# A diffusion trunk layer in fp32 on one core: first stage by blocks of 128 features, one modulation row as a column, six first products ahead of the FFN

## The chip, the core and the metric

The kernel runs on one core of a Trainium2 chip, in one launch. The metric is the device time of that launch in microseconds (us); the runs shown give its median. TensorE is called PE here, VectorE DVE, ScalarE ACT, GpSimd POOL, and SyncE, which here only issues transfers, SP.

## The reference

One layer of a latent diffusion trunk, all fp32, with T = 1024 latent tokens, 256 context tokens, D = 1024 features and a hidden FFN width of 2816:

```
mod   = silu(c) @ w_ada + b_ada          # six vectors of D: sh1 sc1 gt1 sh2 sc2 gt2
mod_c = silu(c_ctx) @ w_ada + b_ada      # the context uses its first two
hc = rmsnorm(ctx, g_pre_mix) * (1 + csc1) + csh1
hl = rmsnorm(x, g_pre_mix) * (1 + sc1) + sh1
states = context_mixer(hc @ w_in)        # only the final scan states
yl = latent_mixer(hl @ w_in, states)     # GLA | 2-D Fourier | conv + RG-LRU
x = x + gt1 * rmsnorm(yl @ w_out, g_post_mix)
hf = rmsnorm(x, g_pre_ffn) * (1 + sc2) + sh2
x = x + gt2 * rmsnorm((silu(hf @ w_gate) * (hf @ w_up)) @ w_down, g_post_ffn)
```

`w_in` has columns for Q, K, V, a decay (DEC), an output gate (OG), the Fourier part (F), and the two inputs of the RG-LRU (RX, RG).

## The kernel before

**Products.** PE multiplies in a reduced format, so every operand is split into a rounded upper half and the rest, its lower half (`split`: ACT casts, DVE or POOL subtracts, line 92), and every product is three matmuls, hi·hi, hi·lo and lo·hi (`mm3`, lines 84 to 86). A row of the trace with L84, L85 or L86 is one of these three, whichever product it belongs to; the name of what is written (`z`, `zn`, `zvc`, `zkc`, `zc`, `o_ps`, `prod`, `dn`) tells which.

**Order and memory.** A scheduler puts the instructions of each engine into an order and inserts the waits. Tiles come from two pools, `pg` (43 tiles of 4 KB per partition) and `hp` (13 of 2 KB), handed out in program order; psum has four banks `mm` and four `aux`. All loads go through SP's queue, in the order in which they stand in the program (`load`); at most eight transfers of the queues are under way at once, since they rotate through eight semaphores.

**First stage** (to about 61 us). Context rows are loaded and normed, `ada_half` computes half of the first two modulation vectors for latent and context tokens from eight loads of 512 KB (64 matmuls with 32 rows, line 154), `columns` brings them into columns, one number per feature (line 200), and `modulate` (lines 189 to 191) turns transposed tokens into `h * scale + shift`, with ACT, and its two halves, with DVE. Context products (`zvc`, `zkc`, then `zc`) are put between the two halves of the modulation; x's rows are loaded behind that, 0 to 3 and then 4 to 7, and transposed (line 181). Then `z_v0` (psum name `zn`), and, later, `z_k` and `z_rx` do the columns V, K and RX of the latent tokens.

**Modulation rows.** Of the other four vectors each is summed by DVE (`ada_row`, line 671, eight steps over D with a load of 512 KB each) and spread over all partitions by two products with ones (`row_ps`, line 682), times a gain row (line 690). This is so for gt1 and for g_pre_ffn·(1 + sc2); the shift sh2 becomes a column by eight small products (`col_ps`, line 676). The calls `ada_step(n)` say where in the program these steps stand: 4, 4, 9, 0, 11, 0. The second row is used in `x_product`, where DVE computes x·(1/rms)·row (line 1034); `x_transposed` (line 1042) transposes that, and ACT adds sh2 as its bias (line 1049). The row for gt2 is summed after block 3 of the FFN.

**FFN's border.** Gate and up products follow Strassen and Winograd: the tokens' two halves of features and of tokens give seven operands, a11, a12, s1, s2, s3, s4, a22 (`operand`, `put`, `sums`), and each of 22 blocks of hidden features has two products with a11 and a12 (`first`) and five with the others (`rest`). `sums(n)` needs tokens n and n + 4, so the last of them wait for the mixer's last rows. Sums and lower halves are made by DVE (lines 937, 1065, 1068) and POOL (1071, 1074, 937). While they run, PE does `first` for `EARLY` = 3 blocks. `t_split` (lines 1122 to 1127) combines the weights of a block for `rest`; their upper halves are called `wa_hi` and `wb_hi`, the weights of `first` `b_hi`. The loop over f then does `rest(f)` with one `first` behind it:

```
    for f in range(NFF):
        new = begun < NFF and begun - f <= (EARLY if f < 2 else EARLY - 1)
        if new:
            ff_gate(begun)
            ff_up(begun)
        wn = t_split(f + 1) if f + 1 < NFF else None
...
        rest(f, w)
        if new:
            ff_b1(begun)
            first(begun)
            begun += 1
```

Of the kernel before, what the change touches and what calls it, by code (L numbers as in the profile page):

```python
# [16 lines left out]
P = 128  # L17
# [21 lines left out]
def tile_trunk(ctx: ExitStack, tc: tile.TileContext, A: dict):  # L39
# [118 lines left out]
    Bcol = pool.tile([P, KB, 2], F32, name="Bcol")  # L158
# [35 lines left out]
    def columns(h, ps):  # L194

        sb = hp((P, 256), name="ada_sb")
        S.copy(sb, ps[:, 0:256])
        pc = (aux if h else mm)("ada_pc")[:, 0:16].rearrange("p (m q) -> p m q", q=8)
        for m in range(2):
            PE.matmul(pc[:, m], sb[:, m * P:(m + 1) * P], sel, start=True, stop=True)  # L200
        pcv = pc.rearrange("p m (i j w) -> p i j m w", i=2, j=2)

        def col4(c0):
            return sml[:, c0 + 4 * h:c0 + 4 * h + 4].rearrange("p (j m) -> p j m", j=2).unsqueeze(3).to_broadcast([P, 2, 2, 2])

        Av, Bv = (t[:, 4 * h:4 * h + 4, :].rearrange("p (j m) w -> p j m w", j=2) for t in (Acol, Bcol))
        V.tensor_add(Av, pcv[:, 1], col4(S_BSC))
        V.scalar_tensor_tensor(Av, Av, 1.0, col4(S_GPM), op0=ALU.add, op1=ALU.mult)
        V.tensor_add(Bv, pcv[:, 0], col4(S_BSH))

    load(cm, A["cmat"])
    cb = [row_block(A["ctx"], i * P) for i in range(2)]
    ada_ps = ada_half(0)
    for xb in cb:
        norm(xb)
    cT = list(transposed(cb))
# [74 lines left out]

    raws = w_N_load([(C_V, 256), (C_DEC, 32)])
    columns(0, ada_ps)
    hc = [[pg((P, 4, TC), F32R, f"hc{s}{i}") for i in range(2)] for s in range(2)]

    def mod_c(h):
        return modulate(cT[4 * h:4 * h + 4], 1, lambda kk: hc[0][kk // 4][:, kk % 4, :], lambda kk: hc[1][kk // 4][:, kk % 4, :])

    mod_c(0)
    w_v = [w_N_split(raws, G)]  # L300
    w_k_raw = [w_T_load(C_K)]
    zvc = [mm("zvc") for _ in range(2)]
    zkc = [mm("zkc") for _ in range(2)]

    def v_c(ks):
        for m in range(2):
            for k in ks:
                mm3(zvc[m][:, 0:288], *(hc[s][k // 4][:, k % 4, m * P:(m + 1) * P] for s in range(2)), *w_v[0][k], k == 0, k == KB - 1)

    v_c(range(4))  # L310
    ada_ps = ada_half(1)
    w_k_raw.append(w_T_load(C_K + P))
    w_k = [split(r, (P, KB, P), eng=G) for r in w_k_raw]
    xb0 = [row_block(A["x"], i * P) for i in range(2)]
    columns(1, ada_ps)
    started = mod_c(1)
    v_c(range(4, KB))
    for p in range(2):
        z_c(w_k[p], range(KB), zkc[p])
    w_rx_raw = w_T_load(C_RX)  # L320
    xb0 += [row_block(A["x"], i * P) for i in range(2, 4)]


    wdec_raw, wdec = hp(name="wdec_raw"), hp((P, 512), F32R, "wdec")
    load(wdec_raw, A["wdec"])
    with tc.issue_after(started.ins):
        S.copy(wdec, wdec_raw)
        V.tensor_sub(wdec[32:64, :], wdec_raw[32:64, :], wdec[32:64, :].bitcast(F32))
        w_rx = [split(w_rx_raw, (P, KB, P))]
        for xb in xb0:  # L330
            norm(xb)
# [33 lines left out]
    for m in range(2):  # L365
        v0_parts(zdt_c, m, vNc[0][:, m, :], zvc[m])
# [1117 lines left out]
```

## Time and profile before

| | before |
|---|---|
| median of 3 runs | 1133.83 us (1131.55 to 1134.39) |
| the profiled execution | 1134.18 us, span 1132.4 us |
| PE busy | 1078.5 us (95%) |
| DVE, ACT, POOL busy | 810.4, 490.2, 83.6 us |
| PE's longest waits | 10.1 us (start), 9.7 us (first block that needs all operands), 5.0 us (modulation row) |

A wait is the idle time of an engine before an instruction, put down to what came last. A row of the timeline is a run of like instructions; its first number is the start, the second the time to the end of the last one. PE's matmuls are pipelined, so the spacing of starts and not a row's length is what one costs.

### The profile page before, as it was taken

What the parts mean: (1) busy time and instruction counts of PE and PEld (TensorE: products, weight loads), DVE (VectorE), ACT (ScalarE), POOL (GpSimd) and SP (SyncE); (2) the same over time, 40 slices, a digit from 0 to 9 for tenths busy, and PEclk for the clock granted to TensorE, in tenths of its full rate; (3) what the DMA queues carried; (4) which work ended last, traced back from release to release, by engine and by line L of the source; (5) the groups of instructions that cost most, each with busy time, mean ns of one, the idle gap of its engine ahead of it and who ended that gap; (6) DMA issues with size and microseconds to landing.
All of it is one profiled execution on the core that took longest, in us unless ns stands there. A gap on an engine that the chain in (4) does not pass through costs nothing.

```text
span 1132.4 us, 15040 instructions
## 1 busy us (share of the span) xinstructions
PE 1078.5 (95%) x5547; PEld 900.1 (79%) x5547; DVE 810.4 (72%) x1370; ACT 490.2 (43%) x931; POOL 83.6 (7%) x93
## 2 busy tenths in 40 slices
PE   4899998999899999959999999999999999999997
PEld 2799896776689888838878888888888888888886
DVE  3474698477588466797879777768777668967794
ACT  3452675466373355663314332333323247554251
POOL 2210000103100011370000000000000000000100
PEclk8899999999999999979999999999999999999999
DMA  9802312222427222361283242424232468767572
GB/s 328 306 20 67 120 38 56 48 56 71 167 75 243 75 93 94 112 167 57 93 276 106 78 136 84 121 75 139 85 114 81 157 218 315 267 216 231 181 283 75
DMA packets 119970, 156.42 MB, mean 138 GB/s; under 512 B 8276, under 2 KB 70996, under 8 KB 119896
## 3 DMA queue, kind: packets, MB, share of 16 engines
q1 hardware_dynamic: 106536, 128.72, 34.9%
q10 hardware_dynamic: 13360, 26.75, 7.0%
q8 instruction: 43, 0.70, 0.3%
q14 instruction: 31, 0.25, 0.1%
HBM read 124.50 MB, written 28.57 MB: 135 GB/s over the span
## 4 chain that ended last, share of the span: by engine, by line
PE 83%; DVE 6%; DMA 4%; ACT 3%; issue 2%; POOL 1%; SPq 0%; DVEq 0%; POOLq 0%; ACTq 0%
PE prod L84 11%; PE prod L85 11%; PE prod L86 11%; PE dn L85 6%; PE dn L84 6%; PE dn L86 6%; PE z L84 3%; PE z L85 3%; PE z L86 3%; PE o_ps L85 3%; PE o_ps L86 3%; PE o_ps L84 3%; PE zn L85 3%; PE zn L86 3%; PE zn L84 2%; DMA wraw<-in_w_in 2%
## 5 line engine op out<-in xcount | busy, mean ns | idle before, releaser
L85 PE MATMUL dn<-dr,dl 128*128 128x512 f32 (+1 forms) x319 | 121.8, 382 | 0.0
L86 PE MATMUL dn<-dr,dl 128*128 128x512 f32 (+1 forms) x319 | 121.8, 382 | 0.0
L84 PE MATMUL dn<-dr,dl 128*128 128x512 f32 (+1 forms) x319 | 118.7, 382 | 0.0
L85 PE MATMUL zn<-w_lo,hl 128*128 128x256 f32 (+1 forms) x256 | 74.1, 292 | 0.0
L84 PE MATMUL zn<-w_hi,hl 128*128 128x256 f32 (+1 forms) x256 | 73.2, 289 | 0.0
L86 PE MATMUL zn<-w_hi,hl 128*128 128x256 f32 (+1 forms) x256 | 72.9, 288 | 0.0
L84 PE MATMUL prod<-a,b_hi 128*128 128x512 f32 x176 | 69.5, 395 | 1.4 <-ACT b_hi L91 1.4
L84 PEld LDWEIGHTS dn<-dr,dl 128*128 128x128 f32 x319 | 60.0, 188 | 11.7
L85 PE MATMUL prod<-a,b_hi 128*128 128x512 f32 x176 | 69.3, 393 | 0.0
L86 PEld LDWEIGHTS dn<-dr,dl 128*128 128x128 f32 x319 | 60.0, 188 | 11.7
L85 PEld LDWEIGHTS dn<-dr,dl 128*128 128x128 f32 x319 | 60.0, 188 | 11.5
L84 PE MATMUL prod<-s,wb_hi 128*128 128x512 f32 x176 | 68.9, 391 | 0.0
L86 PE MATMUL prod<-s,wb_lo 128*128 128x512 f32 x176 | 68.5, 389 | 0.0
L85 PE MATMUL prod<-s,wb_hi 128*128 128x512 f32 x176 | 68.5, 389 | 0.0
L86 PE MATMUL prod<-a,b_lo 128*128 128x512 f32 x176 | 67.9, 390 | 0.0
L84 PE MATMUL z<-hl,w_hi 128*128 128x512 f32 x160 | 65.5, 409 | 1.0 <-ACT on L605 1.0
L85 PE MATMUL z<-hl,w_hi 128*128 128x512 f32 x160 | 64.0, 400 | 0.0
L86 PE MATMUL z<-hl,w_lo 128*128 128x512 f32 x160 | 63.8, 399 | 0.0
L1189 ACT CAST dl<-h 128x512 fp32r<-128x512 f32 x77 | 47.8, 620 | 35.7 <-issue 20.6
L1190 DVE TENSOR_TENSOR dl<-h,dl 128x512 fp32r<-128x512 f32 x77 | 53.3, 692 | 13.6 <-ACT dl L1189 13.6
L1122 ACT CAST b<-wf_raw 128x512 fp32r<-128x512 f32 x22 | 13.7, 622 | 113.6 <-PE prod L86 105.7
L85 PE MATMUL o_ps<-wo_lo,yh 128*128 128x512 f32 x128 | 49.9, 392 | 0.0
(368 smaller groups left out, 2800.8 us busy)
## 6 DMA issues: line engine op xcount, KB each, us to landing
ada_raw<-in_w_ada SPq DMA_DIRECT2D x48, 512.0 KB, 6.3
h<-hd SPq DMA_DIRECT2D x77, 256.0 KB, 5.0
wd_raw<-in_w_down SPq DMA_DIRECT2D x77, 256.0 KB, 4.8
hd<-c ACTq DMA_DIRECT2D x55, 256.0 KB, 2.0
wf_raw<-in_w_gate SPq DMA_DIRECT2D x25, 512.0 KB, 3.9
wf_raw<-in_w_up SPq DMA_DIRECT2D x22, 512.0 KB, 4.4
wraw<-in_w_in SPq DMA_DIRECT2D x16, 512.0 KB, 4.6
xb<-in_x SPq DMA_DIRECT2D x8, 512.0 KB, 8.1
```

The lines of the kernel that those rows point to most:

```text
L84: PE.matmul(out, lh, rh, start=start, stop=False)
L85: PE.matmul(out, lh, rl, start=False, stop=False)
L86: return PE.matmul(out, ll, rh, start=False, stop=stop)
L1122: S.copy(hi, u[:, 4:8])
L1189: S.copy(t[:, 0, :], raw)
L1190: V.tensor_sub(t[:, 1, :], raw, t[:, 0, :].bitcast(F32))
```

## The change

Three parts.

**First stage.** x rows 0 to 3 are loaded first, through ACT's queue. The modulation weights come in eight blocks of 128 features, each two loads (shift and scale) with rows of 512 B, and the columns K and RX of `w_in` in four pairs of blocks of 128 rows. For each block: four transposes, 16 matmuls of 32x128, one small column product, `modulate`, and 12 products into four psum banks, which hold K and RX of the first 512 tokens. The products of the context, a short series of small DVE operations (`softplus`) and the second half of x stand behind that, and splits that POOL did go to DVE.

```
...
+    xb0 = [pg(name="xb") for _ in range(4)]
+    for i, xb in enumerate(xb0):
+        nc.scalar.dma_start(xb, A["x"][i * P:(i + 1) * P, :])
...
+    def ada_load(b):
+
+        raws = []
+        for i in range(2):
+            raw = pg((P, KB, P), name="ada_raw")
+            c = i * D + b * P
+            load(raw, A["w_ada"][:, c:c + P].rearrange("(k p) n -> p k n", p=P))
+            raws.append(raw)
+        return raws
+
+    def ada_part(raws):
+
+        ps = aux("ada_ps")
         for k in range(KB):
-            raw = pg((P, 2, 512), name="ada_raw")
-            load(raw, A["w_ada"][k * P:(k + 1) * P, 0:2 * D].rearrange("p (i n) -> p i n", i=2)[:, :, h * 512:(h + 1) * 512])
             for i in range(2):
-                for j in range(2):
-                    q = 32 * (2 * i + j)
-                    PE.matmul(ps[q:q + 32, 0:256], s32[:, k, :], raw[:, i, j * 256:(j + 1) * 256], start=k == 0, stop=k == KB - 1)
+                g = 32 * (2 * i + k % 2)
+                PE.matmul(ps[g:g + 32, 0:P], s32[:, k, :], raws[i][:, k, :], start=k < 2, stop=k >= KB - 2)
         return ps
...
+    def z_block(b):
+        for (hi, lo), ps in zip(w4, z4):
+            mm3(ps, hi[:, b, :], lo[:, b, :], hl[0][0][b // 2][:, b % 2, :], hl[1][0][b // 2][:, b % 2, :], b == 0, b == KB - 1)
...
+    w4_split()
+    for b in range(KB):
+        kps = [next(x0_T)]
+        columns(b, ada_part(a_raw.pop(b)))
+        modulate(kps, 0, lambda kk: hl[0][0][kk // 2][:, kk % 2, :], lambda kk: hl[1][0][kk // 2][:, kk % 2, :])
+        if b:
+            z_block(b - 1)
+        if b % 2:
+            w4_split()
+    softplus()
+    w_v = [w_N_split(v_raws)]
+    z_block(KB - 1)
...
+    z_v0([0, 1, 2, 3])
     for xb in xb1:
         norm(xb)
+    mod_half(1, xb1)
+    cb = [row_block(A["ctx"], i * P) for i in range(2)]
...
+    z_v0([4, 5, 6, 7])
...
```

PE's order at the start of the program, before: transposes of the context (`xT_ps`), half the modulation (`ada_ps`, 32 rows by 256 features), the column products (`ada_pc`), and then context products.

```order
L181 MATMUL xT_ps<-cm,xb 128x128 x4
L154 MATMUL ada_ps<-ada_raw,s_73 32x256 x4
L181 MATMUL xT_ps<-cm,xb 128x128 x12
L154 MATMUL ada_ps<-ada_raw,s_73 32x256 x28
L200 MATMUL ada_pc<-cm,ada_sb 128x8 x2
L84 MATMUL zvc<-w_hi,hc_219 128x288 x2
L85 MATMUL zvc<-w_lo,hc_219 128x288
```

And now, where `xT_ps` are transposes of x and `z` the products of K and RX:

```order
L196 MATMUL xT_ps<-cm,xb 128x128 x3
L168 MATMUL ada_ps<-ada_raw,s_83 32x128
L196 MATMUL xT_ps<-cm,xb 128x128
L168 MATMUL ada_ps<-ada_raw,s_83 32x128 x15
L214 MATMUL ada_pc<-sel_96,ada_sb 128x4
L196 MATMUL xT_ps<-cm,xb 128x128 x4
L168 MATMUL ada_ps<-ada_raw,s_83 32x128 x16
L214 MATMUL ada_pc<-sel_96,ada_sb 128x4
L196 MATMUL xT_ps<-cm,xb 128x128 x4
L168 MATMUL ada_ps<-ada_raw,s_83 32x128 x14
L84 MATMUL z<-hl_97,w_hi 128x512 x4
```

The first products of the latent tokens now stand right behind the modulation of the third block, and those of the context behind all eight.

**Rows.** g_pre_ffn·(1 + sc2) becomes a column too, and `x_transposed` applies it as ACT's scale; ACT then also does x·(1/rms). The steps stand at 8, 8, 1, 7 and 9, and the row for gt2 at blocks 10 and 11 of the FFN.

```
...
+    def scale_column(ps):
+        g8 = hp((P, P), name="g8")
+        load(g8[0:KB, :], A["g_pre_ffn"].rearrange("(k p) -> k p", p=P))
+        PE.transpose(ps[:, 16:16 + KB], g8[0:KB, :], ident[0:KB, 0:KB])
+        V.tensor_copy(sc2, ps[:, 16:16 + KB])
+        V.scalar_tensor_tensor(sc2, ps[:, 0:KB], 1.0, sc2, op0=ALU.add, op1=ALU.mult)
 
     def all_rows():
         yield from ada_row(2 * D, times_row("g_post_mix", 0.0))
-        yield from ada_row(4 * D, times_row("g_pre_ffn", 1.0))
-        yield from ada_row(3 * D, None)
+        yield from ada_row(4 * D, scale_column, False)
+        yield from ada_row(3 * D, shift_column, False)
...
-            V.scalar_tensor_tensor(xn[:, hs], xr[:, hs], r2, sc2[:, hs], op0=ALU.mult, op1=ALU.mult)
+            S.mul(xn[:, hs], xr[:, hs], r2)
...
-                S.activation(x[:, kk, :], ps[:, k * P:(k + 1) * P], AF.Identity, bias=sh2[:, kk:kk + 1])
+                S.activation(x[:, kk, :], ps[:, k * P:(k + 1) * P], AF.Identity, bias=sh2[:, kk:kk + 1], scale=sc2[:, kk:kk + 1])
...
```

PE's order at the end of the products for RG (`z`), before, where `gate_ps` are the gates of the RG-LRU and `zn` the products with w_og:

```order
L84 MATMUL z<-hl_494,w_hi 128x512
L85 MATMUL z<-hl_502,w_hi 128x512
L86 MATMUL z<-hl_494,w_lo 128x512
L682 MATMUL row_ps<-ada_acc,cm 128x512 x3
L613 MATMUL gate_ps<-uT,gates 128x512 x4
L84 MATMUL zn<-w_hi,hl_487 128x256 x2
L84 MATMUL zn<-w_hi,hl_491 128x256 x2
```

And now:

```order
L84 MATMUL z<-hl_104,w_hi 128x512
L85 MATMUL z<-hl_112,w_hi 128x512
L86 MATMUL z<-hl_104,w_lo 128x512
L653 MATMUL gate_ps<-uT,gates 128x512 x4
L84 MATMUL zn<-w_hi,hl_97 128x256 x2
L84 MATMUL zn<-w_hi,hl_101 128x256 x2
```

The three row products are gone from this place; the two that are left, of gt1, stand ahead of and among the `z` products.

**The FFN's border.** `EARLY` is 6, all sums are made by DVE and in place in the token tiles, in the order a22, s1, s2, s4, s3, and the loop fetches gate and up weights two blocks ahead. Blocks 0 to 3 of the loop have no `first` behind them; `first` of blocks 4 and 5 writes into a `pg` tile.

```
...
-        V.tensor_add(s1, a21, a22)
-        put("s1", n, s1)
+        put("a22", n, a22)
+        V.tensor_add(a22, a21, a22)
+        put("s1", n, a22)
         yield
-        V.tensor_sub(s2, s1, a11)
-        put("s2", n, s2)
+        V.tensor_sub(a21, a11, a21)
+        V.tensor_sub(a11, a22, a11)
+        put("s2", n, a11)
         yield
-        G.tensor_sub(s4, a12, s2)
-        put("s4", n, s4)
-        yield
-        G.tensor_sub(s3, a11, a21)
-        put("s3", n, s3, G)
-        yield
-        put("a22", n, a22, G)
...
+        V.tensor_sub(a12, a12, a11)
+        put("s4", n, a12)
+        put("s3", n, a21)
...
-    EARLY = 3
-    all_of(sums(1))
+    EARLY = 6
+    for _ in range(2):
+        next(s01[1])
     first(0)
-    ff_gate(2)
-    ff_b1(2)
+    for s in s01:
+        all_of(s)
     first(1)
+    ff_gate(3)
+    ff_b1(3)
     x_transposed(TB - 1, xn)
     all_of(sums(2))
+    first(2)
+    ff_gate(4)
+    ff_b1(4)
     s_last = sums(3)
     next(s_last)
-    first(2)
+    first(3)
+    ff_gate(5)
+    ff_b1(5)
     ff_gate(0)
     ff_up(0)
+    all_of(s_last)
+    first(4)
     w = t_split(0)
-    all_of(s_last)
-    for f in range(1, EARLY):
-        ff_gate(f)
-        ff_up(f)
+    first(5)
+    ff_gate(1)
+    ff_up(1)
...
     for f in range(NFF):
-        new = begun < NFF and begun - f <= (EARLY if f < 2 else EARLY - 1)
-        if new:
-            ff_gate(begun)
-            ff_up(begun)
+        if f + 2 < NFF:
+            ff_gate(f + 2)
+            ff_up(f + 2)
...
-        if new:
+        if begun == f + 2 < NFF:
...
```

DVE's order at the end of the sums, now (`hx` are the token tiles, L977 the lower halves, L1158 the sum of a first product, L1168 to L1172 the combinations of a block's weights):

```order
L1111 TENSOR_TENSOR hx<-hx 128x512
L977 TENSOR_TENSOR s_1_4607<-hx,s_0_4605 128x2x128
L977 TENSOR_TENSOR s_1_4608<-hx,s_0_4606 128x2x128
L1168 TENSOR_TENSOR wf_raw<-wf_raw 128x512
L1169 TENSOR_TENSOR b_5014<-wf_raw,b_5014 128x512
L977 TENSOR_TENSOR s_1_4778<-hx,s_0_4776 128x2x128
L1158 TENSOR_TENSOR p_4984<-p_4984,prod 128x512
L977 TENSOR_TENSOR s_1_4779<-hx,s_0_4777 128x2x128
L1170 TENSOR_TENSOR wf_raw<-wf_raw 128x512
L1171 TENSOR_TENSOR wf_raw<-wf_raw 128x512
L1172 TENSOR_TENSOR wf_raw<-wf_raw 128x512
L92 TENSOR_TENSOR wa_lo<-wf_raw,wa_hi 128x1024
```

Every operand's lower half and the combinations stand in one line on DVE ahead of the first lower half that `rest(0)` needs; before, 16 of these subtractions and 8 of the sums were POOL's.

## Rows read from the trace of the kernel before

**Rows 1.** The page's first part: busy time, share of the span, instructions.

```profile
PE 1078.5 (95%) x5547; PEld 900.1 (79%) x5547; DVE 810.4 (72%) x1370; ACT 490.2 (43%) x931; POOL 83.6 (7%) x93
```

**Rows 2.** PE's waits: what waited for what, us in total, times, longest.

```profile
PE xT_ps L181 <- DVE xb L171: 10.1, 1, 10.1
PE prod L84 <- ACT wa_hi L91: 9.7, 1, 9.7
PE row_ps L682 <- DVE ada_acc L671: 5.0, 2, 4.6
```

**Rows 3.** Windows: length; PE, PEld, DVE, ACT, POOL busy; PEclk; DMA share; GB/s.

```profile
20.00:30.00 10.00, 5.33 (x23) 4.89 (x23) 2.84 (x11) 5.06 (x8) 6.36 (x4) 0.52 1.10 347
...
38.00:48.00 10.00, 6.83 (x32) 6.53 (x33) 7.01 (x17) 6.52 (x11) 3.94 (x3) 0.66 1.09 366
48.00:62.80 14.80, 14.80 (x127) 14.80 (x126) 11.04 (x24) 10.18 (x19) 1.09 (x2) 1.00 0.29 97
...
600.00:700.00 100.00, 100.00 (x443) 82.81 (x442) 79.83 (x109) 34.20 (x45) 0.00 (x0) 1.00 0.35 109
```

**Rows 4.** Timeline of PE, first stage: start, us, instruction, records, idle before.

```profile
34.48 1.93 PE L154 MATMUL ada_ps<-ada_raw,s 128*32 128x256 f32 x32
...
42.69 0.44 PE L85 MATMUL zvc<-w_lo,hc 128*128 128x288 f32 x1
42.93 0.44 PE L84 MATMUL zvc<-w_hi,hc 128*128 128x288 f32 x1
...
61.00 0.29 PE L84 MATMUL zn<-w_hi,hl 128*128 128x288 f32 x1
```

**Rows 5.** Instruction groups, one shape each: count, busy us, mean ns, idle before.

```profile
L191 DVE TENSOR_TENSOR hl<-xT,hl 128x512 fp32r<-128x512 f32 x16 | 10.7, 687 | 0.2
...
L190 DVE CAST hl<-xT 128x512 fp32r<-128x512 f32 x16 | 6.5, 423 | 3.2 <-ACT xT L189 3.2
...
L189 ACT ACTIVATE xT<-xT_ps,Bcol,Acol 128x512 f32<-128x512 f32 x16 | 11.3, 778 | 11.5 <-PE xT_ps L181 11.5
```

**Rows 6.** Timeline of PE and ACT around the modulation row.

```profile
301.04 0.39 PE L86 MATMUL z<-hl,w_lo 128*128 128x512 f32 x1
301.26 1.02 PE L682 MATMUL row_ps<-ada_acc,cm 128*128 128x512 f32 x2
...
302.81 1.05 ACT L91 CAST w_hi<-wraw 128x1024 fp32r<-128x1024 f32 x1 [0.69 <-DMA wraw<-in_w_in]
...
306.90 3.68 PE L682 MATMUL row_ps<-ada_acc,cm 128*128 128x512 f32 x4 [4.62 <-DVE ada_acc L671]
310.38 3.63 PE L613 MATMUL gate_ps<-uT,gates 128*128 128x512 f32 x8
...
365.26 1.84 PE L676 MATMUL col_ps<-cm,ada_acc 128*128 128x1 f32 x16
```

**Rows 7.** Timeline of PE at the FFN's border.

```profile
473.32 0.40 PE L84 MATMUL prod<-a,b_hi 128*128 128x512 f32 x1
...
488.41 2.16 PE L1042 MATMUL x_tr<-cm,xn 128*128 128x128 f32 x8 [3.12 <-DVE xn L1034]
...
492.67 0.63 PE L84 MATMUL prod<-a,b_hi 128*128 128x512 f32 x1
493.10 0.63 PE L85 MATMUL prod<-a,b_hi 128*128 128x512 f32 x1
...
508.56 0.79 PE L84 MATMUL prod<-s,wa_hi 128*128 128x512 f32 x1 [9.74 <-ACT wa_hi L91]
```

**Rows 8.** DVE at the border: groups of one shape, and a window.

```profile
L92 DVE TENSOR_TENSOR b_lo<-wf_raw,b_hi 128x1024 fp32r<-128x1024 f32 x22 | 26.9, 1222 | 0.6
...
L937 DVE TENSOR_TENSOR s<-s,s 128x256 fp32r<-128x256 f32 x24 | 17.3, 759 | 0.0
...
L937 DVE TENSOR_TENSOR a<-hx,a 128x256 fp32r<-128x256 f32 x16 | 6.2, 422 | 4.8 <-ACT a L936 4.8
...
500.00:505.00 5.00, 0.00 (x0) 0.00 (x0) 4.96 (x9) 1.31 (x3) 1.21 (x1) 0.66 0.97 231
```

More of the change, by code (lines that the diff above doesn't have):

```diff
@@ L101, in tile_trunk @@
     cm = pool.tile([P, 6, P], F32, name="cm")
+    for i in (0, 5):
+        load(cm[:, i, :], A["cmat"][:, i, :])
     ident, wmask, Cd, Sd, ones = (cm[:, i, :] for i in range(5))
@@ L188, in modulate @@
             f = hp((P, ps.shape[1]), name="xT")
-            i = S.activation(f, ps, AF.Identity, bias=Bcol[:, kk, which:which + 1], scale=Acol[:, kk, which:which + 1])
+            i = S.activation(f, ps, AF.Identity, bias=shsc[:, kk, 0, which:which + 1], scale=Acol[:, kk, which:which + 1])
             V.tensor_copy(hi_of(kk), f)
@@ L192, in modulate, with columns @@
         return i
[L194 to L216, printed above, removed]
+    def columns(b, ps):
+        sb = hp((P, P), name="ada_sb")
+        S.copy(sb, ps[:, 0:P])
+        pc = aux("ada_pc")[:, 0:4]
+        PE.matmul(pc, sb, sel2.rearrange("p i w -> p (i w)"), start=True, stop=True)
+        bias = sml[:, S_BSH:S_BSH + 16].rearrange("p (i k) -> p i k", i=2)[:, :, b:b + 1].to_broadcast([P, 2, 2])
+        V.tensor_add(shsc[:, b], pc.rearrange("p (i w) -> p i w", i=2), bias)
+        V.tensor_scalar(Acol[:, b, :], shsc[:, b, 1, :], 1.0, sml[:, S_GPM + b:S_GPM + b + 1], op0=ALU.add, op1=ALU.mult)
     def w_T_load(c0):
@@ L289, in z_N @@
                 i = 0
[L292 to L331, printed above, removed]
     hl = [[[pg((P, 2, 512), F32R, name=f"hl{s}{h}") for _ in range(4)] for h in range(2)] for s in range(2)]
@@ new lines, in tile_trunk @@
+    softplus()
+    w_v = [w_N_split(v_raws)]
+    z_block(KB - 1)
+    load(cm[:, 1:5, :], A["cmat"][:, 1:5, :])
+    xb1 = [row_block(A["x"], i * P) for i in range(4, 8)]
+    for p in range(2):
+        S.copy(kT[p][:, 0:512], z4[p])
+    for blk in range(2):
+        conv(z4[2 + blk], uT[blk][:, 0:512], blk, 512, 64)
+    wdec_raw, wdec = hp(name="wdec_raw"), hp((P, 512), F32R, "wdec")
+    load(wdec_raw, A["wdec"])
+    S.copy(wdec, wdec_raw)
+    V.tensor_sub(wdec[32:64, :], wdec_raw[32:64, :], wdec[32:64, :].bitcast(F32))
@@ new lines, in tile_trunk @@
+    vN[0][0] = pg((P, 4, 256), name="vN")
+    z_v0([0, 1, 2, 3])
+    for xb in xb1:
+        norm(xb)
+    mod_half(1, xb1)
+    cb = [row_block(A["ctx"], i * P) for i in range(2)]
+    for xb in cb:
+        norm(xb)
+    vN[0][1] = pg((P, 4, 256), name="vN")
+    z_v0([4, 5, 6, 7])
+    hc = [[pg((P, 4, TC), F32R, f"hc{s}{i}") for i in range(2)] for s in range(2)]
+    modulate(transposed(cb), 1, lambda kk: hc[0][kk // 4][:, kk % 4, :], lambda kk: hc[1][kk // 4][:, kk % 4, :])
+    cx = pg((P, 4, TC), name="cx")
@@ new lines, in tile_trunk @@
+    kTc, uTc = cx[:, 0:2, :], cx[:, 2:4, :]
+    for p in range(2):
+        ps = mm("zkc")
+        z_c(w_k[p], range(KB), ps)
+        S.copy(kTc[:, p, :], ps[:, 0:TC])
+    kTcs = hp((P, 2, TC), name="kTcs")
+    exchange(kTcs, kTc)
+    zdt_c = hp((P, 4, 96), name="zdt")
+    for m in range(2):
+        ps = mm("zvc")
+        for k in range(KB):
+            mm3(ps[:, 0:288], *(hc[s][k // 4][:, k % 4, m * P:(m + 1) * P] for s in range(2)), *w_v[0][k], k == 0, k == KB - 1)
+        v0_parts(zdt_c, m, vNc[0][:, m, :], ps)
@@ L407, in tile_trunk @@
+    dec_T(zdt_c, 2, zdec_c[0:96, :])
+    for blk in range(2):
+        ps = mm("zc")
+        z_c(w_rx[blk], range(KB), ps)
+        conv(ps[:, 0:TC], uTc[:, blk, :], blk, TC, TC)
     la_c = pg((P, 2, 2, TC), name="la_c")
@@ L1093, in tile_trunk @@
             xn7 = pg(name="xn")
-            all_of(sums(0))
+            hx6 = pg((P, KB, P), name="hx")
+            ff_gate(2)
+            ff_b1(2)
+            s01 = [sums(0), sums(1)]
+            for _ in range(2):
+                next(s01[0])
     hd = {x: dram.tile([P, NK, 512], F32, name=f"hd{x}") for x in range(1, 8)}
@@ L1391, in tile_trunk @@
         w = wn
-        if f == 3:
-            for _ in ada_row(5 * D, times_row("g_post_ffn", 0.0)):
-                pass
-            gt2 = rows[2]
+        if f == 10:
+            last_row = ada_row(5 * D, times_row("g_post_ffn", 0.0))
+            for _ in range(KB):
+                next(last_row)
+        if f == 11:
+            all_of(last_row)
+            gt2 = rows[1]
     down()
```

149 lines of the change are left out of this document (77 added, 72 removed).

## The prediction

> **What bounds the kernel now.** The page's first part comes first: TensorE (PE) is busy for 95% of the 1132.4 us span, VectorE (DVE) for 72%, ScalarE (ACT) for 43% [rows 1]. A gain has three sources: time in which PE stands still (1132.4 - 1078.5 = 53.9 us), time in which it runs at the lower of its two clocks, and products that needn't be computed; the change takes almost none away. So I read the list of PE's waits next. The reader is to see that its longest three, 10.1, 9.7 and 5.0 us [rows 2], stand at the three places that the change rewrites: the start, the border of the FFN, the spreading of the modulation rows. Each is then read in its own stretch, from windows and timeline; a stall's length is not its worth, because what runs beside it has to be done anyhow.
>
> **First stage, -5 us.** Until 61 us the core fetches modulation weights and does products of the context. DMA is full (share 1.10 and 1.09, 347 and 366 GB/s) while PE is busy for 5.33 and 6.83 of 10 us at a granted clock of 0.52 and 0.66 [rows 3]. Soon after 42.69 us PE is dense; at 61.00 us the first product of the latent tokens starts [rows 4].
> Data: the 16 modulation loads stay 8.4 MB, now by blocks of 128 features; x rows 0 to 3 (2.1 MB) go first, through ACT's queue, ahead of ACT's own work; the columns of K and RX are 2.1 MB, constants 0.4. The last of eight blocks needs 13.0 MB. The new modulation rows are 512 B long; the trace has weights of that row length at 109/0.35 = 311 GB/s, and the full stretch here gives 366/1.09 = 336 [rows 3]. So the last block lands 39 to 42 us after the first issue at 2.5: 41 to 45 us. V's columns (1.2 MB) come 4 us later.
> PE per block at full clock: 12 products at 0.226 us (spacing of 301.04 and 301.26 [rows 6]), 2.7; four transposes, 0.4; 16 modulation matmuls in 32 records, which no row shows in their new shape: 32 take 1.93 us now [rows 4], half as wide then, so 1.0 if width counts and 1.9 if not. I take 1.0, since all other products here scale with width, and 0.5 for the small column product: 4.6. A block's data take 1.31 MB/0.325 = 4.0. ACT needs 0.78 + 0.4 + half a weight cast, 0.5; DVE 0.42 + 0.69 + 0.6 + 0.3 = 2.0 [rows 5]: neither bounds. In the issue order block 0's products stand behind block 2's modulation matmuls, so they start near 21 us, some of them at the lower clock. Eight blocks at 4.3 us, between data and PE, end at 55 us.
> By then 96 products (21.7) and 32 transposes (3.5) are done, 25.2 us of full-clock work. Before had 22.9 at 62.8 us: 144 context products at 0.12 (0.24 at the lower clock, rows 42.69 and 42.93 [rows 4]), 17.4, and 48 transposes and some. So 7.8 us earlier with 2.3 us more: 10 ahead. Given back behind it: x rows 4 to 7 were loaded, transposed and cast under context products; now PE has 5.5 us of transposes and products for DVE's 8 x (0.42 + 0.69) = 8.9, so it waits 3.4, and 1.7 more for the context's first block. Net -5. Bounds: nothing given back, -11; data 4 us later and both waits doubled, +4. POOL's weight splits go to DVE: no cost beside the blocks, where DVE is half idle; 3 us without that cover.
>
> **The rows, -6 us.** At 301.26 us PE does one half row, waits 4.62 us for the second modulation row's sum, spreads it (306.90 to 310.38, 3.5 us) and does the gates in 3.63 us, where 8 records at 0.226 would take 2.0 with the last one's run [rows 6]. A column takes the place of that row: 4.6 + 3.5 + 1.6 = 9.7 go. Added: 16 column records and a transposition, 1.8 by the column that is there already [rows 6]. Late next: the lower halves of w_og. Its upper halves are cast from 302.81, when DMA brings them [rows 6], one modulation load earlier in the queue now; cast 1.05 and subtraction 1.2 end near 305, the gates at 303.2: 1.8 us. Net -9.7 + 1.8 + 1.8 = -6. Bounds: -9 (nothing late), -2 (casts as late as now, gates slow too).
> The multiplication by 1/rms goes from DVE to ACT, which is idle for 57% of the span [rows 1]: zero. It counts only for the last four rows of tokens, where DVE gets 2 us back; they are in the border's list. The row for gt2 moves from block 3 to blocks 10 and 11, where PE is busy for 100 of 100 us and DVE for 79.83 [rows 3]: zero; without that cover some 10 us of DVE.
>
> **The border, -5 us.** PE starts the first products at 473.32 us, stands 3.12 us before the last transposes, and 9.74 us before the block that needs all operands, at 508.56; in the bursts behind a wait the spacing is 0.43 for 0.226 (492.67, 493.10 [rows 7]). Of these 35.2 us three blocks of first products are 72 x 0.226 = 16.3, transposes 1.0: 17.9 uncovered. DVE is the reason: 4.96 of 5 us busy from 500 to 505, PE at 0.00 [rows 8].
> The change gives DVE what POOL did, but takes POOL out of its way: the same 128x256 subtraction takes 759 ns where POOL works beside it (all 24 of them) and 422 without [rows 8]. DVE's list to the first lower half of block 0's weights: 40 lower halves x 0.42 = 16.8; 16 sums x 0.69 [rows 5] = 11.0; six first-product sums, 4.1; four lower halves of weights x 1.22 [rows 8] = 4.9; combinations of weights and the first lower half, 4.7; rest of the mixer's rows, 2.9: 44.4 us. PE has six blocks, 32.6, and 1.0 to cover them: 11 uncovered, 6.5 less than now. Blocks 0 to 3 then have no first products beside them: PE 60 x 0.226 = 13.6 us, DVE 0.798 x 19.0 - 1.9 = 13.3 [rows 3], so 0 to 3 us lost; I take 1.5. Net -5. Bounds: -14 (nearly all covered), +2 (the order puts the fourth weight's lower half so late that the three new blocks wait too).
>
> **Sum.** -5 - 6 - 5 = -16. The profiled execution took 1134.18, which is 0.35 above the median: 1118.2, less 0.35, **1118 us**.
>
> **What speaks against it** is PE's clock. In the stretch from 20 to 30 us PE is fed late, and the granted clock is 0.52: the lower level, 1.2 of 2.4 GHz; from 48 us it runs without gaps, at 1.00 [rows 3]. Products fed block by block, each behind its own DMA and its own chain, could keep the lower level (rival D). The Trainium skill, "TensorE: Matmul & The Clock Gate", section "HAM oscillation — how this bites in real kernels", describes a loop over the contraction that waits for DMA at each step and so runs each step at the lower clock, and advises doing all steps together before a wait, the reverse of this change. By that rule the time would be rival D's; the trace's 0.52 agrees with it. My sum takes the dense state, because 4.6 us of work meets 4.0 us of data per block, so that PE has little to wait for.
>
> **Rivals.**
> B, the first stage gives all it can: x's second half hides under V's products, which DVE, at 11.04 of 14.80 us in that stage now [rows 3], may allow. Then -11 - 6 - 5: 1112; with most of the border's bound, 1103.
> C, a term is empty. The first stage returns what it won, because the context, now covered by modulation's DMA, comes onto the path; or the border's wait only moves: 1123. Both: 1128.
> D, slower: PE stays at 1.2 GHz, because modulation, copy, column, activation, cast and subtraction (1.0 + 0.4 + 0.5 + 0.8 + 0.4 + 0.7 = 3.8 us) follow each other and a block's products wait for them. A block is then 12 x 0.43 = 5.2 and 2.1 of the rest: 7.3 us. The eighth ends at 21 + 58 = 79, 24 later: 1142. It decides from 6.7 us per block (+19: 1137). Against it: the order puts two blocks of modulation between a block's column and its products, and DVE idles.
> E, the column doesn't do what it says: the wait stays under another name, on w_og or on the column itself, since one DVE makes all. The rows give 2: 1122.
>
> **How the numbers follow.** A measurement of this kernel tells 0.3% (3.4 us) from no change: faster is below 1130.4, slower above 1137.2. Forecast with its small errors, 1110 to 1126: 0.47. B 0.15, C with one term 0.13, E 0.06: all faster. C with both terms, up to 1135 with a bound's excess: 0.08, of which 0.02 faster and 0.06 same. D, from mild to full: 0.09, of which 0.02 same and 0.07 slower. All three terms at their upper ends (+4 - 2 + 2: 1138): 0.02, slower. That makes faster 0.83, same 0.08, slower 0.09. The range leaves out D's and the last case's slower part and the end of B: 1101 to 1136.
>
> **What would show it.** First stage: PE dense from about 21 us, granted clock above 0.8 from 25 to 55, the eighth block's last product near 55, then a wait of some 3 us on x's second half; a block of over 6.7 us means D. Rows: no wait over 1 us on a modulation sum near 300 us, gates right behind the z products, one to two us on w_og. Border: six first blocks, waits of about 11 us in all, DVE full, the subtractions at 0.42; waits below 3 us in blocks 0 to 3. I am wrong if subtractions stay near 0.76 without POOL, if DMA falls under 300 GB/s with 512-byte rows, or if a long wait stands at a place not named here.

## The result, and the profile after

The changed kernel takes 1118.51 us (median of four runs, 1116.37 to 1119.34), the kernel before 1133.32 (1131.55 to 1134.39): ratio 0.9868, 95% interval 0.9848 to 0.9888. That is 1.3% or 14.8 us; 1118 was forecast, in a range of 1101 to 1136. The sum was right. Its terms were not, as the two traces show when the same instructions are looked up in both (starts on PE, in us; the profiled executions' spans differ by 15.8 us, their device times by 14.8):

| | before | after | gained so far | by this part | forecast |
|---|---|---|---|---|---|
| first product of the decay (`dec_ps`) | 124.19 | 122.88 | 1.3 | first stage 1.3 | 5 |
| last product with w_og | 377.83 | 370.52 | 7.3 | rows 6.0 | 6 |
| last product of the mixer's output | 473.10 | 468.60 | 4.5 | -2.8 | 0 |
| last down product | 1125.68 | 1109.89 | 15.8 | border and FFN 11.3 | 5 |

The page's first part of the changed kernel, beside [rows 1], and its longest PE waits, beside [rows 2]:

```profile
PE 1079.7 (97%) x5696; PEld 902.2 (81%) x5696; DVE 794.5 (71%) x1394; ACT 506.4 (45%) x953; POOL 46.8 (4%) x64
```

```profile
PE xT_ps L196 <- DVE xb L186: 13.1, 4, 10.2
PE prod L84 <- ACT b_hi L91: 4.2, 1, 4.2
PE z L84 <- DVE hl L205: 2.1, 4, 1.2
```

PE's busy time is 1.2 us more; its idle time falls by 17.0 us, from 53.9 to 36.9. The wait of 9.7 us before the FFN and that on a modulation row are gone; the one at the start is longer, and one of 4.2 us on first-product weights is new.

The first stage in windows, beside [rows 3] (busy us of PE, PEld, DVE, ACT, POOL; PEclk; DMA share; GB/s):

```profile
20.00:30.00 10.00, 9.62 (x77) 6.68 (x70) 4.72 (x8) 2.86 (x5) 0.00 (x0) 1.00 1.16 294
30.00:38.00 8.00, 7.71 (x82) 6.13 (x81) 3.34 (x8) 2.77 (x4) 0.00 (x0) 1.00 1.11 305
...
62.80:100.00 37.20, 37.19 (x291) 36.55 (x290) 25.47 (x67) 19.26 (x37) 4.15 (x6) 1.00 0.03 6
```

and in the timeline of PE:

```profile
19.28 1.94 PE L168 MATMUL ada_ps<-ada_raw,s 128*32 128x128 f32 x32
...
24.93 2.08 PE L84 MATMUL z<-hl,w_hi 128*128 128x512 f32 x4
...
32.87 1.08 PE L168 MATMUL ada_ps<-ada_raw,s 128*32 128x128 f32 x32
...
54.45 1.20 PE L84 MATMUL z<-hl,w_hi 128*128 128x512 f32 x4 [0.35 <-DVE hl L205]
...
58.90 1.20 PE L84 MATMUL z<-hl,w_hi 128*128 128x512 f32 x4 [1.21 <-DVE hl L205]
...
61.75 0.29 PE L84 MATMUL zn<-w_hi,hl 128*128 128x288 f32 x1
```

PE is nearly always busy from 18 us, but until about 27 us at half its pace: 32 modulation records take 1.94 us, later 1.08. The first products of blocks 0, 6 and 7 start at 24.93, 54.45 and 58.90 us, so blocks 0 to 5 take 4.9 us each; V's products start at 61.75, where 55 was forecast. Behind them PE is busy for 37.19 of 37.20 us: no wait there.

The rows [rows 6] and the border [rows 7] after:

```profile
299.77 0.39 PE L86 MATMUL z<-hl,w_lo 128*128 128x512 f32 x1
300.00 3.59 PE L653 MATMUL gate_ps<-uT,gates 128*128 128x512 f32 x8
303.03 1.04 PE L84 MATMUL zn<-w_hi,hl 128*128 128x256 f32 x4
...
325.29 0.36 PE L893 MATMUL fc_ps<-fcol,cm 128*128 128x2 f32 x2 [1.17 <-DVE fcol L881]
...
329.26 1.84 PE L716 MATMUL col_ps<-cm,ada_acc 128*128 128x1 f32 x16
...
484.00 1.27 PE L1082 MATMUL x_tr<-cm,xn 128*128 128x128 f32 x8 [1.29 <-ACT xn L1074]
...
492.22 0.79 PE L84 MATMUL prod<-a,b_hi 128*128 128x512 f32 x1 [4.20 <-ACT b_hi L91]
...
494.88 0.80 PE L86 MATMUL prod<-a,b_lo 128*128 128x512 f32 x1 [0.58 <-DVE b_lo L92]
...
512.09 0.39 PE L84 MATMUL prod<-s,wa_hi 128*128 128x512 f32 x1
```

The gates stand right behind the z products. From the first of the first products (468.91) to the first block that needs all operands (512.09, below "the first full block") are 43.2 us, where before had 35.2, and there is no wait before the latter. The windows of these two stretches, before and then after, columns as above:

```profile
473.32:508.56 35.24, 21.30 (x89) 16.57 (x88) 34.62 (x49) 24.05 (x71) 24.34 (x22) 0.80 0.54 149
```

```profile
468.91:512.09 43.18, 37.11 (x154) 29.32 (x152) 37.19 (x79) 32.87 (x81) 4.62 (x2) 0.92 0.38 111
```

DVE was busy for 34.6 of 35.2 us; now it is for 37.2 of 43.2, and ACT for 32.9 in place of 24.1.

### The profile page after: what moved, and what is told of

Same layout as the page of the kernel before. It is cut to its first block, busy times and chain, and to the rows that moved or that the text cites. A ratio compares the mean times of both kernels' runs of the same rounds, so it can differ in the third digit from the quotient of the medians.

```text
span 1116.6 us, 15349 instructions
## 1 busy us (share of the span) xinstructions
PE 1079.7 (97%) x5696; PEld 902.2 (81%) x5696; DVE 794.5 (71%) x1394; ACT 506.4 (45%) x953; POOL 46.8 (4%) x64
## 4 chain that ended last, share of the span: by engine, by line
PE 89%; ACT 4%; DVE 3%; DMA 1%; issue 1%; POOL 1%; DVEq 0%; POOLq 0%; ACTq 0%
PE prod L86 12%; PE prod L84 12%; PE prod L85 12%; PE dn L84 6%; PE dn L86 6%; PE dn L85 6%; PE z L84 3%; PE z L85 3%; PE z L86 3%; PE o_ps L86 3%; PE o_ps L84 3%; PE o_ps L85 3%; PE zn L85 3%; PE zn L86 3%; PE zn L84 3%
## 5 line engine op out<-in xcount | busy, mean ns | idle before, releaser
L84 PE MATMUL z<-hl,w_hi 128*128 128x512 f32 x160 | 63.0, 419 | 3.2 <-DVE hl L205 2.1
L85 PE MATMUL z<-hl,w_hi 128*128 128x512 f32 x160 | 63.9, 400 | 0.0
L1191 ACT ACTIVATE c<-c 128x512 f32<-128x512 f32 x22 | 13.9, 633 | 85.9 <-DVE c L1190 82.8
```

The costliest lines, as they stand in the source:

```text
L84: PE.matmul(out, lh, rh, start=start, stop=False)
L85: PE.matmul(out, lh, rl, start=False, stop=False)
L1191: S.activation(c21, c21, AF.Silu)
```

## The experiments

All were timed in five rounds beside the kernel before, which took 1132.7 in the first group of four, 1134.3 in the second, 1133.9 in the group of three and 1133.1 with the last. So that one kernel moved by 1.6 us from group to group, and where two kernels of different groups are compared below, a difference of one or two us is not clear of noise. Behind each time stand its ratio to the kernel before and the 95% interval of that.

**The parts one by one.** First, the changed kernel with the first stage of before:

```
-    xb0 = [pg(name="xb") for _ in range(4)]
...
+    ada_ps = ada_half(0)
...
-        columns(b, ada_part(a_raw.pop(b)))
...
+    mod_half(1, xb1)
+    ada_step(4)
```

> The changed kernel with the first stage of before (context first, modulation in two halves); rows and border stay changed. Theory, from the two traces: the new first stage is worth little, since the decay's first product starts only 1.3 us earlier than before; so this kernel takes 1118.5 + 1.3 = about 1120 us. Rival, by the prediction's term: the stage is worth 5 us, and something behind it hides that: 1123 to 1124. Second rival: it is worth nothing or less, 1117 to 1118.5.

Measured: 1120.01 us (ratio 0.9884, 0.9871 to 0.9896). That is 1.5 us behind the changed kernel, with intervals that overlap: the first stage is worth some 1.5 us, not 5. Its decay product starts at 123.59, 0.7 later than in the changed kernel; its border is 1.0 us longer (44.2 for 43.2), its output products are 1.1 us shorter. One trace is a rough measure of that first landmark: in the four traces with the old first stage it lies between 123.14 and 124.19, in five with the new one, unchanged, between 122.06 and 122.88. The means, 123.7 and 122.4, are again 1.3 apart.

Then before with the rows alone:

```
-        yield from ada_row(4 * D, times_row("g_pre_ffn", 1.0))
+        yield from ada_row(4 * D, scale_column, False)
...
-            V.scalar_tensor_tensor(xn[:, hs], xr[:, hs], r2, sc2[:, hs], op0=ALU.mult, op1=ALU.mult)
+            S.mul(xn[:, hs], xr[:, hs], r2)
```

> The kernel before with the rows alone changed (the scale of the FFN's norm as a column, 1/rms by ACT, steps at their new places). Theory: the wait of 4.6 us, two row products and slow gates go and a second set of column products comes: -6 us, about 1127. Rival: the column's sum or the weights behind it bring a wait of their own: -2, about 1131.

Measured: 1125.67 (0.994, 0.9926 to 0.9955), -7. By the landmarks 6.4 us are gained up to the last product with w_og; 1.05 of them lie ahead of the decay, where this kernel does what before does, so the rows have 5.3. At the border the first full block starts 31.3 us after the first products, for 35.2 before, where DVE has the multiplications less. But ACT, which got the multiplications, is late twice:

```profile
PE x_tr L1052 <- ACT xn L1044: 3.8, 1, 3.8
...
PE o_ps L84 <- ACT yh L956: 2.0, 1, 2.0
```

And before with the border alone (`EARLY`, `sums`, `put`, the loop and the place of gt2's row):

```
-    EARLY = 3
-    all_of(sums(1))
+    EARLY = 6
+    for _ in range(2):
+        next(s01[1])
```

> The kernel before with the border of the FFN alone changed (six first products, all sums by DVE in place, loop two blocks ahead, row for gt2 later). Theory, from the two traces: PE's span from the first of the first products to the last product before the down projection is 11.4 us shorter, less some 2 us lost in the mixer's output products: about -9 to -11, 1122 to 1124. Rival, the prediction's term of -5: about 1128.

Measured: 1121.48 (0.9897, 0.9885 to 0.991), -11.2. Alone the two parts give 7.1 and 11.2, together (the first run) 12.7. By the landmarks, 3.9 us of what the rows gave alone lay at the border, in the same DVE list that the border part clears. They relieve the same place, so it is paid at most once; in fact less comes of it: with both, the stretch from the first products to the first full block is 44.2 us, not 40.7 as with the border alone, and the wait on the fourth block's weights 4.2, not 2.4. That the multiplications, now ACT's, cause it is the next guess; a run below tries it.

**What sets the pace of the blocks.** PE warmed up:

```
+    warm = aux("warm")
+    for _ in range(18):
+        PE.matmul(warm, smask[:, 0:P], smask, start=True, stop=True)
```

> The changed kernel with 18 products of a constant tile in fp32, 128x512, put ahead of PE's first transposes, results unused. In the changed kernel's trace 32 modulation records take 1.94 us until about 25 us and 1.08 from 32 us on. Theory: PE's lower clock in its first 15 us sets the pace of the first blocks, not DMA; warmed up it starts block 0's products earlier and the eighth block ends some 4 to 6 us before 61.6: 1113 to 1115. Rival: DMA, which moves 284 to 312 GB/s there, sets the pace; PE then waits for modulation weights instead, and the time stays within 1 us of 1118.5. Second rival: the products delay the first transposes: 1119 to 1121.

Measured: 1119.36 (0.9876, 0.9862 to 0.989). This is the second rival's number, and doesn't tell the other two apart: the 18 products lasted until 20.0 us, 5 us beyond the last normed row, and what the clock gave, the delay took; the eighth block starts at 58.81, as without them. So 12:

```
-    for _ in range(18):
+    for _ in range(12):
```

> As the run with 18 constant products ahead of PE's first transposes, with 12. With 18 they lasted until 20.0 us, 5 us past the last normed row, and block 0's products started at 24.17 us all the same (24.93 without). With 12 they should end near 14 us, before the last transpose is ready at 15.1. Theory: PE, which then shows no idle time over 0.3 us and 5.0 us per block, sets the pace of the blocks; at full clock from 15 us block 0's products start near 19 to 20 us and the eighth block ends near 56 to 57: 1113 to 1115. Rival: arrival of data sets the pace; block 0's products start early, but PE then waits for modulation weights, the eighth block ends at 60 to 62 as now: within 1 us of 1118.5.

Measured: 1119.89 (0.9873, 0.986 to 0.9887): not the theory's number, and 0.4 us above the rival's range. The timeline of PE and a window of the eighth block have the reason:

```profile
15.51 1.07 PE L171 MATMUL ada_ps<-ada_raw,s 128*32 128x128 f32 x30
...
18.67 1.07 PE L171 MATMUL ada_ps<-ada_raw,s 128*32 128x128 f32 x30 [0.50 <-DMA ada_raw<-in_w_ada]
...
22.27 1.07 PE L171 MATMUL ada_ps<-ada_raw,s 128*32 128x128 f32 x28 [0.93 <-DMA ada_raw<-in_w_ada]
...
57.58 1.81 PE L84 MATMUL z<-hl,w_hi 128*128 128x512 f32 x4 [1.85 <-DVE hl L208]
59.19 0.63 PE L85 MATMUL z<-hl,w_hi 128*128 128x512 f32 x1
59.62 0.63 PE L86 MATMUL z<-hl,w_lo 128*128 128x512 f32 x1
...
62.05 0.29 PE L84 MATMUL zn<-w_hi,hl 128*128 128x288 f32 x1
```

```profile
57.00:62.00 5.00, 4.42 (x12) 3.49 (x13) 2.75 (x6) 3.70 (x8) 1.10 (x2) 0.66 0.05 19
```

The modulation runs at full pace from 15.5 us, and now PE waits for DMA. The eighth block starts at 57.58 instead of 58.90, behind a wait of 1.85 us on DVE's half of its own operand. But behind that wait its products are 0.43 us apart, at a granted clock that stands at the lower of its two levels for much of the window (mean 0.66), and V's products start at 62.05, 0.3 later than in the changed kernel: what the start won, the clock at the end took back. So I changed the loads and nothing else: the weights of two blocks per load.

```
-            raw = pg((P, KB, P), name="ada_raw")
...
-            load(raw, A["w_ada"][:, c:c + P].rearrange("(k p) n -> p k n", p=P))
...
+                raw = pg((P, 4, 256), name="ada_raw")
...
+                load(raw, A["w_ada"][512 * j:512 * (j + 1), c:c + 256].rearrange("(k p) n -> p k n", p=P))
```

> The changed kernel with the modulation weights of two blocks per load, so rows of 1 KB for 512 B, as many loads of the same size. Theory that PE sets the pace: DMA gets faster (over the 284 to 312 GB/s of now, towards the 336 to 366 of the stage before), but the eighth block ends where it did, within 1 us of 1118.5. Rival, that DMA sets the pace: the eighth block ends 3 to 5 us earlier, 1114 to 1116.

Measured: 1119.14 (0.9867, 0.9853 to 0.988). Two windows of this kernel, and its PE at the start:

```profile
20.00:30.00 10.00, 9.61 (x87) 6.79 (x78) 4.99 (x9) 2.64 (x5) 0.00 (x0) 1.00 1.10 349
30.00:38.00 8.00, 6.82 (x87) 4.96 (x86) 3.65 (x9) 3.03 (x5) 0.00 (x0) 1.00 1.11 350
```

```profile
18.96 1.89 PE L169 MATMUL ada_ps<-ada_raw,s 128*32 128x128 f32 x32
...
22.05 0.65 PE L169 MATMUL ada_ps<-ada_raw,s 128*32 128x128 f32 x16
22.62 1.20 PE L84 MATMUL z<-hl,w_hi 128*128 128x512 f32 x4
```

DMA moves 349 GB/s for 294, and the eighth block starts 1.7 us earlier (57.23). That can't be put down to DMA alone: in this trace PE is at full pace from about 21 us on, some 6 us sooner than in the changed kernel's. The gain is lost at the border, whose order the scheduler made anew (45.0 us for 43.2). Then both, with V's split kept behind the eighth block's activation:

```
...
-    w_v = [w_N_split(v_raws)]
+    with tc.issue_after(started.ins):
+        w_v = [w_N_split(v_raws)]
     z_block(KB - 1)
```

> Three edits of the first stage together: 12 constant products ahead of PE's transposes, modulation weights with rows of 1 KB, and the split of V's weights held behind the last block's activation. Alone, the first moved the eighth block's products from 58.9 to 57.6 us and the second to 57.2. Theory: PE's clock (until 28 us) and DMA (290 GB/s) bound the blocks in turn, so only both together move it: the eighth block starts at 52 to 54 us, 1113 to 1115. Rival: the chain through ACT and DVE or PE's 5.0 us per block holds it: 56 to 57 us, 1116 to 1118.

Measured: 1115.51 (0.9842, 0.9829 to 0.9855). The timeline of PE:

```profile
18.09 1.08 PE L172 MATMUL ada_ps<-ada_raw,s 128*32 128x128 f32 x32
...
53.67 1.20 PE L84 MATMUL z<-hl,w_hi 128*128 128x512 f32 x4
```

The eighth block starts at 53.67, without a wait, and the decay's first product at 119.43, 3.5 us before the changed kernel's; of the 5.2 us at the eighth block 1.3 are lost to a new wait before V's products. The time is 0.5 above the theory's range, and its interval overlaps the changed kernel's; the decay's start is clear of the 122.06 to 122.88 of the kernels with the stage unchanged.

What the edits move, and what they don't, stands in the starts of the blocks' first products:

| | block 0 | block 6 | block 7 | per block, 0 to 6 |
|---|---|---|---|---|
| changed kernel | 24.93 | 54.45 | 58.90 | 4.92 |
| 12 products ahead | 23.26 | 52.61 | 57.58 | 4.89 |
| rows of 1 KB | 22.62 | 52.77 | 57.23 | 5.03 |
| all three edits | 21.34 | 50.50 | 53.67 | 4.86 |

The pace of the blocks is the same in all four, at 294 GB/s and at 349, and PE is busy for 7.71 of 8 us in the changed kernel's window from 30 to 38: it is PE's own work, the 4.6 us of the prediction and 0.3 more. Clock and DMA decide when block 0 starts, and the chain through ACT and DVE what the last step costs. Which share the third edit has wasn't tried.

**What holds the border.** First products of three blocks instead of six:

```
-    EARLY = 6
+    EARLY = 3
...
-    first(3)
-    ff_gate(5)
-    ff_b1(5)
...
-    first(4)
     w = t_split(0)
-    first(5)
```

> The changed kernel with three first products ahead of the FFN's loop and not six; sums, their order and places stay. Theory, the prediction's: PE has 16 us less to do while DVE makes the operands, and gets 6 us of DVE's list back: +8 to +10, 1127 to 1129. Rival: the gain of the border is that POOL no longer slows DVE, and six blocks matter little: +0 to +3, 1118 to 1122.

Measured: 1129.27 (0.9949, 0.9935 to 0.9962), 10.8 slower than the changed kernel. A wait and a window:

```profile
PE prod L84 <- ACT wa_hi L91: 14.3, 1, 14.3
...
500.00:510.00 10.00, 5.64 (x12) 4.01 (x13) 10.00 (x20) 4.94 (x11) 0.00 (x0) 0.50 0.03 7
```

Up to 504.02 us PE has nothing to do, and DVE is full: without the three more blocks nothing is left of the border's gain. The time is even 3.6 us above that of the run with the rows alone, which has the old border and the old first stage: all sums by DVE, with only three blocks to cover them, cost more than POOL's share did. POOL again for 16 of 40 lower halves:

```
...
-        put("a22", n, a22)
+        put("a22", n, a22, G)
...
-        put("s3", n, a21)
+        put("s3", n, a21, G)
```

> The changed kernel with the lower halves of a22 and s3, 16 of 40, made by POOL again. Theory: POOL's work slows DVE's subtractions of the same shape from 0.42 to some 0.76 us, as before, so that 24 of them take as long as 40 did: no gain, 0 to +5 us, 1118 to 1124. Rival: the slow ones before had another cause (other tiles, sums not in place), DVE keeps 0.42 and has 6.7 us less to do: 1114 to 1118.

Measured: 1121.99 (0.9897, 0.9884 to 0.9911), 3.5 slower, by intervals that just overlap. Its timeline of DVE and POOL:

```profile
477.00 0.68 DVE L1101 TENSOR_TENSOR hx<-hx 128x512 f32<-128x512 f32 x1
...
491.64 1.21 DVE L1101 TENSOR_TENSOR hx<-hx 128x512 f32<-128x512 f32 x1
...
494.42 0.95 DVE L977 TENSOR_TENSOR s<-hx,s 128x256 fp32r<-128x256 f32 x1
```

```profile
489.14 3.16 POOL L977 TENSOR_TENSOR s<-hx,s 128x256 fp32r<-128x256 f32 x4
...
494.09 1.88 POOL L977 TENSOR_TENSOR s<-hx,s 128x256 fp32r<-128x256 f32 x2 [1.79 <-ACT s L976]
```

One sum takes 0.68 us with none of these on POOL and 1.21 beside POOL, one subtraction 0.95 for 0.42; POOL takes 0.97 us for each of its own. All subtractions named s, here (24 on DVE) and then in the changed kernel (all 32):

```profile
L977 DVE TENSOR_TENSOR s<-hx,s 128x256 fp32r<-128x256 f32 x24 | 11.1, 495 | 2.8 <-ACT s L976 2.8
```

```profile
L977 DVE TENSOR_TENSOR s<-hx,s 128x256 fp32r<-128x256 f32 x32 | 12.4, 421 | 2.6 <-ACT s L976 2.6
```

against the 759 ns of [rows 8]. The four of the 24 that fall into POOL's intervals take 0.76 to 0.96 us, the other 20 0.41 to 0.43. So the rival, another cause of the slow ones, is out. But the theory's sum is out too: 20 stay fast, DVE has less to do, and the kernel is slower all the same. Two waits have grown or come:

```profile
PE prod L84 <- ACT b_hi L91: 6.1, 1, 6.1
```

```profile
DVE hx L1101 <- POOL a L977: 2.0, 2, 1.3
```

A sum in place overwrites a tile that POOL's subtraction still reads, so DVE now waits for the slower engine, and the fourth block's weights come later (4.2 in the changed kernel).

1/rms back to DVE:

```
-            S.mul(xn[:, hs], xr[:, hs], r2)
+            V.tensor_scalar_mul(xn[:, hs], xr[:, hs], r2)
```

> The changed kernel with the multiplication by 1/rms done by DVE (one operand and one number per partition) and not by ACT. The part with rows alone gained 8.5 us and the border alone 12.8 by their traces, together less than the sum; in the joined kernel PE waits 4.2 us on an upper half of first-product weights and 1.3 on this multiplication, both made by ACT. Theory: ACT, which the rows part loads with 16 multiplications, is now the engine that holds the border: these two waits shrink, -2 to -3 us, about 1116. Rival: DVE is the bound there, as the prediction had it: same or up to 2 us slower, 1118 to 1121.

Measured: 1117.55 (0.9855, 0.9842 to 0.9869). 1 us below the changed kernel, with intervals that overlap; the waits at the border stay (4.0 and 1.2). Not the -2 to -3 of the theory, and no difference that is clear of noise. So the multiplications aren't what makes the two parts together gain less at the border than the border alone; what does is open. The fourth block's weights one place earlier:

```
+    ff_gate(3)
+    ff_b1(3)
     for s in s01:
         all_of(s)
     first(1)
-    ff_gate(3)
-    ff_b1(3)
```

> The changed kernel with the fourth block's first-product weights loaded and split one place earlier, ahead of the second half of the sums. Theory: what PE waits for at the border of the changed kernel is no more DVE's list but the place of this upper half in ACT's order (wait 4.2 us, 0.6 on the lower half, then 2.6 at the lower clock): these go and nothing is behind them, -4 to -6 us, 1113 to 1115. Rival, the prediction's: DVE's list of 44 us is the bound; the wait moves to the first block that needs all operands, 1117 to 1119.

Measured: 1116.25 (0.985, 0.9836 to 0.9864), -2.3, by intervals that overlap. At most half of the theory; by the trace the border is 1.4 us shorter (41.8 for 43.2). The wait is now 2.8 us on the next weights and 0.8 before the first full block: it moves along the list of ACT and DVE and shrinks, but doesn't go. Last, the edits of the first stage, of 1/rms and of the fourth block together:

> All that helped, together: the three edits of the first stage, 1/rms by DVE, the fourth block's weights one place earlier. Theory, that these are separate places: 1118.5 - 3.0 - 1.0 - 2.3 = about 1112. Rival: the two edits at the border act on the same waits (ACT's order), and only one of them counts: 1113 to 1115.

Measured: 1115.58 (0.984, 0.9827 to 0.9854), above theory and rival and no better than the first stage's edits alone. The first products start at 464.74 us, 4.2 earlier than in the changed kernel and 1.2 earlier than with the stage's edits, but:

```profile
506.19 0.79 PE L84 MATMUL prod<-s,wa_hi 128*128 128x512 f32 x1 [3.45 <-ACT wa_hi L91]
506.79 0.63 PE L85 MATMUL prod<-s,wa_hi 128*128 128x512 f32 x1
507.21 0.63 PE L84 MATMUL prod<-s,b 128*128 128x512 f32 x1
```

The wait stands before the first full block again, the rival of the run before, and behind it 14 starts are 0.40 to 0.59 us apart for 0.227: 2.9 us more. The lowest median is that of the changed kernel with the three edits of the first stage: 1115.51, 3.0 below the changed kernel, by intervals against before that overlap by a little.

## Why the prediction was right, and where it wasn't

**First stage: forecast -5, measured -1.3 to -1.5.** Three terms failed, two of them against the third. "They start near 21 us, some of them at the lower clock. Eight blocks at 4.3 us" failed first: the start was at 24.93, everything until 27 us ran at half pace, and a block took 4.9 us, since PE's own 4.6, not DMA's 4.0, sets the pace. DMA gave 284 to 312 GB/s where I had put 325, below the 300 that I had named as a sign of being wrong. The eighth block ended at 61.7, 6.7 us late. I had let width set the modulation's price (right: 1.08 us for 32 records) and had not asked at what clock they would run. The second is "Before had 22.9 at 62.8 us": that sum, context products and 48 transposes, is the work up to about 61.5 and leaves out the products of V, which run from 61.00 on [rows 4]; and the 144 context products cost 18.2 us at the spacing of the new trace, not 17.4. At 61.75 before had done 24.1 us of work; the changed kernel had done 25.4 there, at the same prices. The 1.3 between them is what arrives at the decay. The third is "Given back behind it", 5 us: PE shows no wait there, since V's products cover x's second half, which is what rival B said.

Rival D didn't come: a block took 4.9 us, not 6.7. But its mechanism has a part in it, at the start. That the half pace is PE's clock and not late data is shown by the run with 12 products, in which the same 30 records take 1.07 us. The Trainium skill, "TensorE: Matmul & The Clock Gate", section "HAM oscillation — how this bites in real kernels", has a loop that drops to the lower clock at every step; here the pace held from 28 us on, with a wait of 0.3 us in every second block, and fell in the run with 12 products, behind the single wait of 1.85 us.

**Rows: forecast -6, measured -6.0,** with small errors that cancel. From the first row product to the gates 9.1 us went: the wait of 4.6, the 3.5 behind it and 1.0 for the first half row, which my sum had left out. The gates take 3.03 us now, 3.07 before: that they had been slowed by 1.6 was wrong, since their records start 0.43 us apart in both traces, and 0.226, the price of another product, didn't hold for them. The wait of 1.8 on w_og didn't come; no wait stands before its products. A second set of column products came, 1.9 us for 1.8 forecast, and 0.7 more of waiting on a column of the Fourier part (1.17 for 0.43).

**The mixer's output products: forecast zero, measured +2.8.** Of this 0.8 is a set of transposes that stood behind the first products before. The rest is spacing: 384 products at 0.233 us where before had 0.228. The moved multiplication isn't its cause: with the rows alone, where ACT does it, the spacing is 0.228, and with it back on DVE it is 0.233. The border alone has 0.229, both parts with the old first stage 0.230, and all ten kernels with the new first stage have 0.233, though that part changes nothing in these products. Why is open.

**Border: forecast -5, measured -11.3.** Six blocks to cover DVE's work and 0.42 us per subtraction came as forecast, and the run with three blocks shows that they carry the gain. The bound did not come as forecast. DVE's list, put at 44.4 us, kept DVE busy for 37.2 in these 43.2 us, because its instructions follow each other at less than their own length (subtractions of 0.42 us start 0.34 apart). DVE isn't full, as it was before; it and ACT wait for each other, and PE stands 4.2 us on an upper half that is ACT's, at the place where the bound "+2" had expected a lower half. So 9.5 us uncovered (43.2 less 32.7 of products and 1.0) are near the 11 of the forecast by some luck. Before had 17.9 by the same count: 8.4 less, 0.8 of it by the transposes that moved, where 6.5 was forecast (17.9 less 11 is 6.9). "0 to 3 us lost; I take 1.5" in blocks 0 to 3: nothing, PE is busy for 60.00 of 60 us from 520 on. And I left out what lies behind 508.56: 1.6 us of slow spacing after the long wait, which is gone, and about 1 us in small gaps around gt2's row, which I had priced at zero.

So the total was right by luck: 3.7 us too much in the first stage and 2.8 us that were not expected to be lost at the output stand against 6.3 too little at the border.

## What to carry to other kernels

Sum and terms are two claims: look up the same instructions in both traces before saying why a forecast held. Parts that relieve the same list of work are paid at most once, so price them together; and a wait that is taken away early can come back where the list ends, and behind a long one (4.2 and 3.5 us here) the products ran at the lower clock. When the start of a stage hangs on clock and DMA and its end on a chain, one edit alone may not show in the time: look where each block starts, and try the edits together before calling any of them idle.

## What the runs showed that I had not expected

The column of granted clocks reads 1.00 for the first 27 us of the changed kernel, while the same records take 1.94 us and later 1.08, and 1.07 in the same place with products ahead of them. The trace's records of the clock begin at 27.4 us there, with full clock (at 6.8 with 12 products ahead), and what lies before the first record reads 1.00. So at the start of these programs the spacing tells the clock and that column doesn't. DMA moved 284 to 312 GB/s with rows of 512 B and 348 to 350 with rows of 1 KB, at the same size of load. And kernels that differ only in the first stage differ by up to 1.8 us at the border: 43.2 us in the changed kernel, 44.4 with 12 products ahead and 45.0 with rows of 1 KB, where the scheduler put DVE's instructions of the border into another order.
